# First head group's context features made among the value and receptance projections

## The chip, the cores and the metric

The kernel runs on one core of a Trainium2 chip. The metric is the device time of one execution in microseconds (us), lower is better. PE is TensorE (PEld its weight loads), DVE VectorE, ACT ScalarE, POOL GpSimd, and SP the engine that here only issues loads of weights. A queue named SP, ACT or POOL is the one on which that engine issues its DMAs.

## What is computed

The reference is a model of two blocks of two layers each, in fp32, on 256 tokens and 256 context tokens of width 1024. The change is in the second layer of the first block, whose mixer is an RWKV (a linear recurrence with a decay for each channel, in both directions, 16 heads of 64):

```python
def rwkv_features(h, ...):
    xx = centred_shift(h);  mix = lambda j: h + xx * mu[j]
    xw, xk, xv, xa = mix(1), mix(2), mix(3), mix(4)
    k = xk @ wk;  v = heads(xv @ wv)
    kk = normalized heads(k * k_k)
    for d in range(2):
        w_raw = heads(w0[d] + jnp.tanh(xw @ w1[d]) @ w2[d])
        decay = jnp.exp(-jnp.exp(-jax.nn.softplus(-w_raw) - 0.5))
        a = jax.nn.sigmoid(heads(a0[d] + (xa @ a1[d]) @ a2[d]))
        k_d = kh * (1 + (a - 1) * k_a_h)
    r = heads(mix(0) @ wr);  g = jax.nn.sigmoid(mix(5) @ g1) @ g2
# scan over the 256 context tokens from zero, then over the 256 tokens from the state left:
    S = S * w_t - (S @ kk_t) (kk_t * a_t) + v_t k_t;   y_t = S @ r_t
# both directions summed, normalized, plus a bonus, times g, then @ wo; then a residual and an MLP
```

The layer's modulation (shift, scale, gate) and that of layers behind it are products of a vector with matrices of 1024 x 6144.

## The kernel before

Products of fp32 are split into a high and a low half and made by three matmuls (lines 187 to 189); the halves of a weight tile are made by ACT (L161) and DVE (L164). Weights come as loads `wraw` on SP's queue (L151). A scheduler orders each engine's instructions beforehand; the order of the code gives it their priorities, and the pools the buffers that they wait for.

The mixer `odd1` runs in two phases. The first makes the mixes and the projections: key, value and receptance, each 1024 x 1024, with results going to memory (`kT_dram`, `kkn_dram`, `v_dram`, `rT_dram`), and three low-rank products, `lora(1)` to `twl` beside key and `lora(4)`, `lora(5)` to `tal`, `sgl` behind value. Each `lora` mixes all eight k tiles in `rw_raw` (L683) into one buffer `mixr` and then runs eight matmuls (L744).

The second phase works in four head groups: group 0 is context tokens of heads 0 to 7, group 1 the tokens of the same heads, groups 2 and 3 the same for heads 8 to 15. A group has four steps:

- **Features** (`rw_open`, then `rw_feat` for four head pairs, each with two directions; one head pair and direction is called a piece here, eight a group). A piece has two low-rank matmuls into a PSUM tile `lo` (L989) with `w2s` and `a2s`, loaded once a group on ACT's queue (L967); activations and products on ACT and DVE; four transposes of `BK` (L1046), eight products of `BK` with `ARc` (context) or `ARx` (tokens) in two tiles (L1056), and masks that write `AB` (L1069). `KB`, and `ARx` and `RB` for tokens, go to memory.
- **Inverse** (`rw_inv`): four copies of `AB` to `ND` on ACT (L1092), a transpose to `NS`, and 31 steps of two operations on DVE (L1101, L1102); then `rw_post` reassembles it on PE (L1122 and on).
- **Chain** (`rw_chain`): four steps, each with products of `UV` with `AB` (`begin`, L172), a copy `rhs` (L1214), 16 products with the inverse (L1220), the state `St`, and for tokens the outputs, which need `ard` and `rbd` reloaded.
- The next group's features are called from `ahead`, at places of a table `pos`.

Behind the chains comes the readout (L898, L938, L955), then the wo projection.

`self.side` is work of other places: twenty units of modulation products with vectors (L203). A unit is eight matmuls from four loads of 512 KB; two buffers hold them. `tick` advances it at places given by a table `tk`: at each piece of features, and after each L1220 batch. One tick is one load with its two matmuls. What is left over, `do(side)` runs behind the chains. In an execution a matmul has two records, so eight matmuls are x16 in the trace.

Of the kernel before, what the change touches and what calls it, by code (L numbers as in the profile page):

```python
# [9 lines left out]
F32 = mybir.dt.float32  # L10
# [3 lines left out]
ALU = mybir.AluOpType  # L14
# [649 lines left out]
class L1(K):  # L664
# [14 lines left out]
    def rw_raw(self, h, xx, mu, j, T):  # L679

        m = self.T(self.pp, [P, KT, T2], "mixr", bufs=1)
        for k in range(KT):
            self.nc.vector.scalar_tensor_tensor(m[:, k, :T], xx[:, k, :T], mu[:, j, k:k + 1], h[:, k, :T], ALU.mult, ALU.add)  # L683
        return m[:, :, :T]

    def odd1(self, xs, cst, Acol, Bcol):
# [27 lines left out]

        with self.phase(ns2=6) as ph:
# [17 lines left out]
            hsum = self.T(self.pp, [P, 4, 8], "hsum")  # L733
            nc.gpsimd.dma_start(hsum, A["k_hsum"])
            hexp = self.T(self.pp, [8, 4, P], "hexp")
            nc.gpsimd.dma_start(hexp, A["k_hexp"])

            def lora(j, n, T, dst):
                w = self.T(self.pp, [P, KT, P], "lw", bufs=1)
                nc.scalar.dma_start(w, A["lora1"][n])  # L740
                m = self.rw_raw(h, xx, mu, j, T)
                ps = self.psum((P, T))
                for k in range(KT):
                    nc.tensor.matmul(ps, w[:, k, :], m[:, k, :], start=k == 0, stop=k == KT - 1)  # L744
                if j == 5:
                    nc.scalar.activation(dst, ps, AF.Tanh, scale=0.5)
                    nc.vector.tensor_scalar(dst, dst, 0.5, 0.5, ALU.mult, ALU.add)
                else:
                    for d in range(2):
                        q = slice(64 * d, 64 * d + 64)  # L750
                        nc.scalar.activation(dst[q, d, :], ps[q], AF.Tanh if j == 1 else AF.Copy)

            for u in range(2):
# [3 lines left out]
                def sink(j, ps):  # L757
                    k = u * 4 + j
                    kt = self.T(self.pp, [P, T2], "kt", bufs=4)
# [10 lines left out]
                rn = self.T(self.pp, [8, T2], "rn", bufs=1)  # L770
# [3 lines left out]
                for j in range(4):  # L774
                    k = u * 4 + j
                    pb = self.T(self.pa, [P, T2], "ada")
                    nc.tensor.matmul(pb, hexp[:, j, :], rn, start=True, stop=True)
                    kn = self.S2([P, T2])
                    nc.vector.scalar_tensor_tensor(kn, kts[j], par[:, 4, k:k + 1], pb, ALU.mult, ALU.mult)
                    nc.scalar.dma_start(kknd[k], kn)  # L780
            for u in range(2):
# [10 lines left out]
            lora(4, 1, T2, tal)  # L792
            lora(5, 2, S, sgl)
            xr = self.rw_mixes(h, xx, mu, 0, S)
            for u in range(2):
                def sink(j, ps, u=u):
                    t = self.S2([P, S])
                    nc.scalar.activation(t, ps, AF.Copy)
                    nc.scalar.dma_start(rTd[u * 4 + j], t)
                self.lin_T(xr, A["wr"], u, S, sink)  # L800

# [11 lines left out]
        bon = self.T(rk, [P, 2, 16], "bon")  # L813
# [4 lines left out]
        with self.phase((3, 2, 1), 0) as ph:  # L818
# [3 lines left out]
            E3 = [self.T(gp, [P, 4, 65], f"E3{d}") for d in range(2)]  # L822
            for c in range(2):
                nc.gpsimd.memset(St[c], 0.0)
                nc.gpsimd.memset(E3[c][:, :, 64 * c:64 * c + 1], 1.0)
            E = dict(E3=E3, kT=kTd, kkn=kknd, rT=rTd, St=St, twl=twl, tal=tal, hpar=hpar, hka=hka, vd=vd,
                     ms=mstrict, mi=mincl, rmask=rmask, yd=yd, Y1=Y1, bon=bon, rkI=rkI, kbd=[self.tc.dram_tile([2, 4, P, 4, P], F32, name=f"kb_dram{g}") for g in range(4)],
                     ard=[self.tc.dram_tile([2, 4, P, 4, P], F32, name=f"ar_dram{g}") for g in range(2)],
                     rbd=[self.tc.dram_tile([2, 4, P, 8, 64], F32, name=f"rb_dram{g}") for g in range(2)])
            st = None  # L830
            self.nq = 4
            F = self.rw_open(0, False, gp)
            for hp in range(4):
                self.rw_feat(hp, gp, E, F)
            for g in range(4):
                N = {"hp": 0}

                def ahead(p):

                    while g < 3 and N["hp"] < 4 and self.pos[g][N["hp"]] <= p:  # L840
                        if N["hp"] == 0:
                            N["F"] = self.rw_open((g + 1) // 2, g % 2 == 0, gp)
# [115 lines left out]
    def rw_open(self, G, isx, gp):  # L958
# [4 lines left out]
        F["gC"] = self.T(gp, [P, 4, 2, 4], "gC", bufs=3)  # L963
# [6 lines left out]
    def rw_feat(self, hp, gp, E, F):  # L970
# [15 lines left out]
        for d in range(2):  # L986
            pwa = self.T(self.pl, [P, 2, S], "lo")
# [28 lines left out]
            ar = self.T(gp, [P, 4, P if isx else 64], "ARx" if isx else "ARc", bufs=3 if isx else 16)  # L1016
# [1069 lines left out]
```

## Time and profile before

| | us |
|---|---|
| timed runs | 2262.54, 2259.03, 2252.01 |
| their median | 2259.03 |
| the profiled execution | 2250.88 |
| its span | 2248.9 |
| PE busy in the span | 2075.3 (92%) |
| DVE, ACT, POOL busy | 1159.6, 856.6, 119.8 |

The span is what the profiler sees from the first to the last instruction. All rows below come from that one execution; their starts are us from the span's start. Stages by those starts: key about 673 to 734, value with the low-rank products to 817, receptance to 841, group 0's features to 905, the first inverse with features of groups 1 and 2 to 1014, chains to 1287, wo from 1293. Idle time of PE is what the stages are read for, since it is busy most of the span.

### The profile page before, as it was taken

To read this page: it belongs to the slowest core of one execution; us is meant where nothing else is said; L and a number is where in the kernel's file an instruction comes from. 1 tells how busy PE (TensorE), PEld (TensorE's weight loads), DVE (VectorE), ACT (ScalarE), POOL (GpSimd) and SP (SyncE) were. 2 spreads that over 40 slices of the span, in tenths; PEclk is the share of its full clock that TensorE was granted. 3 is DMA by queue.
4 is the path that set the end of the run, shared out by engine and by line. 5 is a ranking of instruction groups with operands and counts; after the bars stand their busy time and mean duration, and the time that the engine had idled before them with its cause. 6 is when DMAs were issued, how large, how long until landed. Compare 5 with 4: busy or idle time off the path is not lost. (4 is left out here: it accounts for less than half of the span.)

```text
span 2248.9 us, 32827 instructions
## 1 busy us (share of the span) xinstructions
PE 2075.3 (92%) x13114; PEld 1451.2 (65%) x13114; DVE 1159.6 (52%) x2419; ACT 856.6 (38%) x1650; POOL 119.8 (5%) x216
## 2 busy tenths in 40 slices
PE   7999899999989989899997789998998989999897
PEld 4864688888866675685652569987765439646542
DVE  2247543433465536866826265666664236475433
ACT  3334443322352446564432345544452114243211
POOL 0100000000021000001111100000000000010000
PEclk9999999999999998759897889999998999999898
DMA  7448212222332426736886555537464959452494
GB/s 285 142 186 322 76 73 94 94 94 94 113 128 89 140 100 211 228 92 200 263 280 192 177 217 183 187 118 272 171 252 163 386 202 354 156 206 96 179 383 173
DMA packets 124310, 414.53 MB, mean 184 GB/s; under 512 B 20608, under 2 KB 59152, under 8 KB 88432
## 3 DMA queue, kind: packets, MB, share of 16 engines
q1 hardware_dynamic: 59824, 340.03, 41.1%
q10 hardware_dynamic: 55552, 50.95, 7.3%
q0 software_dynamic: 8768, 21.31, 3.1%
q8 instruction: 107, 1.75, 0.3%
q14 instruction: 59, 0.48, 0.1%
HBM read 383.30 MB, written 28.93 MB: 183 GB/s over the span
## 5 line engine op out<-in xcount | busy, mean ns | idle before, releaser
L164 DVE TENSOR_TENSOR wlo<-wraw,whi 128x1024 fp32r<-128x1024 f32 x252 | 308.0, 1225 | 405.6 <-ACT whi L161 398.3
L161 ACT ACTIVATE whi<-wraw 128x1024 fp32r<-128x1024 f32 x252 | 265.4, 1058 | 490.2 <-PE mm L189 234.6
L187 PE MATMUL mm<-hT_h,whi 128*128 128x256 f32 (+1 forms) x832 | 268.2, 333 | 2.3 <-ACT whi L161 2.3
L188 PE MATMUL mm<-hT_l,whi 128*128 128x256 f32 (+1 forms) x832 | 267.3, 328 | 0.0
L189 PE MATMUL mm<-hT_h,wlo 128*128 128x256 f32 (+1 forms) x832 | 242.2, 327 | 0.5 <-DVE wlo L164 0.3
L203 PE MATMUL ada<-wraw,csil 128*32 128x512 f32 x768 | 148.1, 663 | 30.7 <-DMA wraw<-in_bda 19.7
L187 PEld LDWEIGHTS mm<-hT_h,whi 128*128 128x128 f32 x832 | 157.4, 191 | 19.8 <-ACT whi L161 4.0
L188 PEld LDWEIGHTS mm<-hT_l,whi 128*128 128x128 f32 x832 | 158.6, 191 | 14.9
L189 PEld LDWEIGHTS mm<-hT_h,wlo 128*128 128x128 f32 x832 | 149.2, 190 | 16.3 <-DVE wlo L164 1.5
L188 PE MATMUL mm<-wlo,b 128*128 128x512 f32 x384 | 151.3, 394 | 0.1
L189 PE MATMUL mm<-whi,b 128*128 128x512 f32 x384 | 150.8, 393 | 0.0
L1934 PE MATMUL ada<-wraw,mo_xd 128*64 128x512 f32 x512 | 135.5, 599 | 0.0
L187 PE MATMUL mm<-whi,b 128*128 128x512 f32 x384 | 135.1, 393 | 0.0
L310 PE MATMUL tr<-s,x 128*128 128x128 f32 x288 | 57.0, 342 | 50.4 <-DVE s L301 20.0
L188 PE MATMUL mm<-wlo,hT_h 128*128 128x512 f32 (+1 forms) x256 | 98.8, 388 | 1.4 <-DVE wlo L164 1.4
L189 PE MATMUL mm<-whi,hT_l 128*128 128x512 f32 (+1 forms) x256 | 95.9, 388 | 0.0
L187 PE MATMUL mm<-whi,hT_h 128*128 128x512 f32 (+1 forms) x256 | 95.3, 398 | 0.5 <-ACT whi L161 0.4
L310 PEld LDWEIGHTS tr<-s,x 128*128 128x128 f32 x288 | 48.9, 240 | 62.0 <-issue 33.7
L188 PEld LDWEIGHTS mm<-wlo,b 128*128 128x128 f32 x384 | 72.0, 188 | 17.9 <-DVE wlo L164 0.8
L187 PEld LDWEIGHTS mm<-whi,b 128*128 128x128 f32 x384 | 72.0, 188 | 16.6
L189 PEld LDWEIGHTS mm<-whi,b 128*128 128x128 f32 x384 | 72.0, 188 | 16.4
L1934 PEld LDWEIGHTS ada<-wraw,mo_xd 128*64 128x64 f32 x512 | 38.1, 136 | 67.9 <-issue 67.7
(520 smaller groups left out, 3714.6 us busy)
## 6 DMA issues: line engine op xcount, KB each, us to landing
wraw<-in_w SPq DMA_DIRECT2D x64, 1024.0 KB, 4.8
wraw<-in_moe_gu SPq DMA_DIRECT2D x64, 1024.0 KB, 7.8
wraw<-in_ada SPq DMA_DIRECT2D x32, 1024.0 KB, 7.2
wraw<-in_moe_d SPq DMA_DIRECT2D x32, 1024.0 KB, 7.1
wraw<-in_bda SPq DMA_DIRECT2D x48, 512.0 KB, 4.7
wraw<-in_bda SPq DMA_DIRECT2D x24, 1024.0 KB, 4.8
wraw<-in_ada SPq DMA_DIRECT2D x32, 512.0 KB, 4.8
wraw<-in_b_in SPq DMA_DIRECT2D x12, 1024.0 KB, 11.5
```

What stands on the lines that cost most here:

```text
L161: nc.scalar.activation(h, src, AF.Copy)
L164: nc.vector.tensor_tensor(l, src, h.bitcast(F32), ALU.subtract)
L187: mm(ps, ah, bh, start=first, stop=False)
L188: mm(ps, ah, bl, start=False, stop=False)
L189: mm(ps, al, bh, start=False, stop=last)
L203: i = nc.tensor.matmul(ps[q:q + 32, :], lhs[:, k, :], raw[:, j % self.wn, :], start=k < nq, stop=k >= 8 - nq, tile_position=(0, q))
L310: nc.tensor.matmul(pt[:, j, :], xs[e + j][:, k * P:(k + 1) * P], dall[:, e + j, :], start=True, stop=True)
L1934: nc.tensor.matmul(pg[64 * e:64 * e + 64, :], xd[:, k, s0:s0 + 64], gu[e](k), start=k == 0, stop=k == KT - 1, tile_position=(0, 64 * e))
```

## The change

Group 0's features (`rw_open` and four calls of `rw_feat`) are called in the first phase: two head pairs ahead of value, one behind each half of value. `lora(4)` and `lora(5)` are called ahead of value. The buffers that only key and the low-rank products use (`hsum`, `hexp`, `lw`, `mixr`, `kt`, `rn`) lie in a pool `kp`, which is released then; the features' work buffers lie in a pool `fw` that follows, released behind receptance. What outlasts the phase (`E3`, and group 0's `AB`, `gC`, `ARc`) lies in a pool `fp`, which group 3 uses again later. `rw_raw` goes; `mixr` is four buffers of one k tile. The `lo` tile of group 0's features is taken from the PSUM buffers named `ada`. The first phase has two weight buffers (`self.weights(2)`) where it had four. During the first phase `self.at` is `"end"` and `side` isn't set, so the ticks of group 0's features advance nothing; the side work begins in the second phase as `late_side`.

```diff
@@ odd1
+        fp = pool(name="fp", bufs=1)
+        E3 = [self.T(fp, [P, 4, 65], f"E3{d}") for d in range(2)]
...
+        self.weights(2)
         with self.phase(ns2=6) as ph:
...
-            hsum = self.T(self.pp, [P, 4, 8], "hsum")
+            kp = tc.alloc_tile_pool(name="kp", bufs=1, reuse_waits="tile")
+            hsum = self.T(kp, [P, 4, 8], "hsum")
...
             def lora(j, n, T, dst):
-                w = self.T(self.pp, [P, KT, P], "lw", bufs=1)
+                w = self.T(kp, [P, KT, P], "lw", bufs=1)
                 nc.scalar.dma_start(w, A["lora1"][n])
-                m = self.rw_raw(h, xx, mu, j, T)
                 ps = self.psum((P, T))
                 for k in range(KT):
-                    nc.tensor.matmul(ps, w[:, k, :], m[:, k, :], start=k == 0, stop=k == KT - 1)
+                    m = self.T(kp, [P, T2], "mixr", bufs=4)[:, :T]
+                    nc.vector.scalar_tensor_tensor(m, xx[:, k, :T], mu[:, j, k:k + 1], h[:, k, :T], ALU.mult, ALU.add)
+                    nc.tensor.matmul(ps, w[:, k, :], m, start=k == 0, stop=k == KT - 1)
...
+            lora(4, 1, T2, tal)
+            lora(5, 2, S, sgl)
+            kp.release()
+            fw = tc.alloc_tile_pool(name="fw", bufs=1, reuse_waits="tile")
+            self.pl, self.lo = self.pa, "ada"
+            F = self.rw_open(0, False, fp, fw)
+            for hp in range(2):
+                self.rw_feat(hp, fw, E, F)
             for u in range(2):
...
                 self.lin_tok(xv, A["wv"][u], range(4), sink)
-            lora(4, 1, T2, tal)
-            lora(5, 2, S, sgl)
+                self.rw_feat(2 + u, fw, E, F)
             xr = self.rw_mixes(h, xx, mu, 0, S)
...
                 self.lin_T(xr, A["wr"], u, S, sink)
+            fw.release()
...
+            self.lo = "lo"
+            self.at, self.side = "unit", self.late_side
             st = None
-            self.nq = 4
-            F = self.rw_open(0, False, gp)
-            for hp in range(4):
-                self.rw_feat(hp, gp, E, F)
...
-                            N["F"] = self.rw_open((g + 1) // 2, g % 2 == 0, gp)
+                            N["F"] = self.rw_open((g + 1) // 2, g % 2 == 0, fp if g == 2 else gp, gp)
@@ rw_open, rw_feat
-        F["AB"] = self.T(gp, [P, 64, 64], "AB", bufs=3)
+        F["AB"] = self.T(fp, [P, 64, 64], "AB", bufs=1 if fp is not gp else 2)
...
-            pwa = self.T(self.pl, [P, 2, S], "lo")
+            pwa = self.T(self.pl, [P, 2, S], self.lo)
...
-            ar = self.T(gp, [P, 4, P if isx else 64], "ARx" if isx else "ARc", bufs=3 if isx else 16)
+            ar = self.T(gp if isx else F["pool"], [P, 4, P if isx else 64], "ARx" if isx else "ARc", bufs=3 if isx else 8)
@@ layer1
-        self.at, self.side = "unit", chain(self.gates(1, 0), self.mods(1, 1), self.gates(1, 1), self.ada2(0))
+        self.at, self.late_side = "end", chain(self.gates(1, 0), self.mods(1, 1), self.gates(1, 1), self.ada2(0))
```

Lines of the features and chains stand six further down in the changed kernel (L989 is L995, L1046 L1052, L1056 L1062, L1220 L1226), L744 is L749, L798 is L810, L938 L943, L898 L903.

How the engines' rows move. PE before, behind receptance: the last receptance matmuls (L187 to L189), then the low-rank matmuls of the first pieces with side matmuls (L203) among them.

```order
L188 MATMUL mm_5665<-mixl_5527,whi_5754 128x256
L189 MATMUL mm_5665<-mixh_5526,wlo_5755 128x256
L989 MATMUL lo_5862<-twl_4498,w2s_5854 128x256
L989 MATMUL lo_5862<-tal_4499,a2s_5856 128x256
L203 MATMUL ada_5869<-wraw_5870,csil_6_86 32x512 x2
L989 MATMUL lo_5919<-twl_4498,w2s_5854 128x256
L989 MATMUL lo_5919<-tal_4499,a2s_5856 128x256
L989 MATMUL lo_5975<-twl_4498,w2s_5854 128x256
L989 MATMUL lo_5975<-tal_4499,a2s_5856 128x256
L1046 MATMUL tr_5895<-ident_67,BK_5890 128x128 x4
L1056 MATMUL tr_5903<-ARc_5891,BK_5890 128x64 x4
```

These L989, L1046 and L1056 are group 0's; in the changed kernel none of them is left here.

PE after, in the second half of the value projection (`mm` and `mixh` are value's product and mix): a piece's low-rank matmuls, transposes and products now lie between its rows.

```order
L995 MATMUL ada_5372<-twl_4498,w2s_5228 128x256
L995 MATMUL ada_5372<-tal_4499,a2s_5230 128x256
L189 MATMUL mm_5417<-whi_5508,mixl_5102 128x512
L187 MATMUL mm_5418<-whi_5508,mixh_5101 128x512
L188 MATMUL mm_5418<-wlo_5509,mixh_5101 128x512
L1052 MATMUL tr_5260<-ident_67,BK_5255 128x128 x4
L1062 MATMUL tr_5268<-ARc_5256,BK_5255 128x64 x4
L189 MATMUL mm_5418<-whi_5508,mixl_5102 128x512
L187 MATMUL mm_5419<-whi_5508,mixh_5101 128x512
L188 MATMUL mm_5419<-wlo_5509,mixh_5101 128x512
L189 MATMUL mm_5419<-whi_5508,mixl_5102 128x512
```

Eight pieces stand so among value and receptance, and no L203 stands among them. The first row behind receptance is an L172 on `UV`, sixteen in all, and then L995 of group 1.

ACT before, behind receptance (L798 are its last copies): the loads of `w2s` and `a2s`, then those of the first features.

```order
L798 ACTIVATE s_1145_5788<-mm_5664 128x256
L798 ACTIVATE s_1146_5791<-mm_5665 128x256
L967 DMA w2s_5854<-in_w2s 128x512
L799 DMA rT_dram<-s_1145_5788 128x256
L799 DMA rT_dram<-s_1146_5791 128x256
L967 DMA a2s_5856<-in_a2s 128x512
L980 DMA kTl_5858<-kT_dram 128x256
L982 DMA kknl_5860<-kkn_dram 128x256
L980 DMA kTl_5971<-kT_dram 128x256
L982 DMA kknl_5973<-kkn_dram 128x256
```

The first UV load (L1178) follows these, and the `ND` copies stood some 60 us further on.

ACT after, at the same place (L810 are the same copies, `ND` the copies for the first inverse, `UV` the first chain's start):

```order
L810 ACTIVATE s_1278_6210<-mm_6086 128x256
L810 ACTIVATE s_1279_6213<-mm_6087 128x256
L1098 ACTIVATE ND_6262<-AB_5226 32x1024 x4
L1184 DMA UV_6514<-v_dram_4505 64x512
L811 DMA rT_dram<-s_1278_6210 128x256
L811 DMA rT_dram<-s_1279_6213 128x256
L1184 DMA UV_6516<-v_dram_4506 64x512
L1184 DMA UV_6600<-v_dram_4505 64x512
L1184 DMA UV_6602<-v_dram_4506 64x512
L973 DMA w2s_6631<-in_w2s 128x512
L973 DMA a2s_6633<-in_a2s 128x512
```

The `ND` copies and the `UV` loads have moved ahead of `w2s` and `a2s`, which are now group 1's.

SP before, at the end of the chains (`in_bda0` are side loads of 512 KB, `in_wo` and `in_w1_1` weights of 1 MB):

```order
L151 DMA wraw_1831_8777<-in_bda0 128x1024
L151 DMA wraw_1832_8781<-in_bda0 128x1024
L151 DMA wraw_2172_10632<-in_wo 128x2048
L151 DMA wraw_2177_10666<-in_wo 128x2048
L151 DMA wraw_2182_10700<-in_wo 128x2048
L151 DMA wraw_2187_10734<-in_wo 128x2048
L151 DMA wraw_2240_10910<-in_w1_1 128x2048
L151 DMA wraw_2245_10968<-in_w1_1 128x2048
```

Here the whole side work has been loaded before wo.

SP after, at the same place:

```order
L151 DMA wraw_1963_9475<-in_bda0 128x1024
L151 DMA wraw_1975_9518<-in_bda0 128x1024
L151 DMA wraw_2194_10668<-in_wo 128x2048
L151 DMA wraw_2199_10702<-in_wo 128x2048
L151 DMA wraw_2204_10736<-in_wo 128x2048
L151 DMA wraw_2209_10770<-in_wo 128x2048
L151 DMA wraw_2262_10947<-in_w1_1 128x2048
L151 DMA wraw_2267_11005<-in_w1_1 128x2048
L151 DMA wraw_1991_9578<-in_bda0 128x1024
L151 DMA wraw_1992_9582<-in_bda0 128x1024
L151 DMA wraw_2280_11087<-in_w1_1 128x2048
```

Two side loads, `wraw_1991` and `wraw_1992`, now stand behind four loads of wo and two of the MLP.

PE before, behind the last L1220 batch (the L172 end its outputs):

```order
L172 MATMUL mm_10426<-UV_10341,rbd_10347 64x64
L172 MATMUL mm_10426<-UV_10343,rbd_10351 64x64
L938 MATMUL tr_10574<-y_1_1152_5818,rwc_4484 128x512
L955 MATMUL tr_10589<-g_1154_5820,sgl_4504 128x512
L187 MATMUL mm_10628<-whi_10634,moh_2148_10555 128x512
L187 MATMUL mm_10629<-whi_10634,moh_2148_10555 128x512
L938 MATMUL tr_10593<-y_1_1152_5818,rwc_4484 128x512
L188 MATMUL mm_10628<-wlo_10635,moh_2148_10555 128x512
L189 MATMUL mm_10628<-whi_10634,mol_2150_10557 128x512
```

The wo projection follows the outputs with only the readout's L938 and L955 between.

PE after, at the same place; the last two L203 use those two side loads (here without the first of their numbers):

```order
L217 MATMUL ada_9468<-adp_9466,sel_4_76 2x512
L203 MATMUL ada_9474<-wraw_9475,csil_16_107 32x512 x2
L203 MATMUL ada_9474<-wraw_9518,csil_16_107 32x512 x2
L203 MATMUL ada_9474<-wraw_9578,csil_16_107 32x512 x2
L203 MATMUL ada_9474<-wraw_9582,csil_16_107 32x512 x2
L217 MATMUL ada_9604<-adp_9602,sel_4_76 2x512
L903 MATMUL tr_10595<-ident_67,z_1281_6237 128x128 x4
L903 MATMUL tr_10602<-ident_67,z_1281_6237 128x128 x4
L187 MATMUL mm_10664<-whi_10670,moh_2170_10591 128x512
L188 MATMUL mm_10664<-wlo_10671,moh_2170_10591 128x512
L187 MATMUL mm_10665<-whi_10670,moh_2170_10591 128x512
```

Side matmuls, their selections (L217) and eight transposes of `z` (L903) now stand ahead of the wo projection, where it came after readout rows. In all, of the 160 side matmuls in PE's row, 32 stood ahead of the first L1220 batch and none behind the sixteenth; now none stands ahead of the first, and twelve behind the sixteenth. L1122, the first inverse's reassembly, stood behind some 14 pieces of groups 1 and 2, and now behind nine. At the first L1220 batch all 16 context pieces and half a token piece of group 3 had been passed, now 12.

## Rows read from the trace of the kernel before

**Rows 1.** The windows view by stage: busy us (instructions) per engine, TensorE's granted clock, DMA share, GB/s.

```profile
734.00:817.00 83.00, 79.43 (x275) 50.55 (x275) 36.45 (x50) 32.97 (x49) 0.00 (x0) 0.98 0.38 135
...
841.00:905.00 64.00, 56.16 (x304) 35.04 (x304) 37.03 (x89) 37.70 (x101) 3.90 (x8) 0.84 0.72 226
...
1014.00:1287.00 273.00, 233.72 (x3331) 139.09 (x3331) 148.30 (x351) 100.10 (x178) 36.77 (x69) 0.89 0.72 226
1287.00:1314.00 27.00, 19.55 (x114) 14.23 (x114) 21.26 (x31) 14.93 (x21) 0.00 (x0) 0.95 0.87 359
```

**Rows 2.** The timeline of PE behind receptance: start us, duration us, instruction, [idle before <-releaser].

```profile
840.30 0.28 PE L189 MATMUL mm<-mixh,wlo 128*128 128x256 f32 x1
844.23 1.19 PE L989 MATMUL lo<-twl,w2s 128*128 128x256 f32 x2 [3.65 <-DMA w2s<-in_w2s]
847.18 1.19 PE L989 MATMUL lo<-tal,a2s 128*128 128x256 f32 x2 [1.77 <-DMA a2s<-in_a2s]
```

**Rows 3.** The timeline of PE in the first group's features, one piece.

```profile
873.68 0.70 PE L989 MATMUL lo<-twl,w2s 128*128 128x256 f32 x2
...
874.75 1.10 PE L1056 MATMUL tr<-ARc,BK 64*128 64x64 f32 x8
875.78 0.66 PE L1046 MATMUL tr<-ident,BK 128*128 128x128 f32 x4
```

**Rows 4.** The timeline of PE in the second context group's features, one piece.

```profile
966.61 1.22 PE L989 MATMUL lo<-twl,w2s 128*128 128x256 f32 x2
...
968.61 1.97 PE L1056 MATMUL tr<-ARc,BK 64*128 64x64 f32 x8
970.51 1.11 PE L1046 MATMUL tr<-ident,BK 128*128 128x128 f32 x4
```

**Rows 5.** The windows view of three other stretches.

```profile
867.00:918.00 51.00, 48.92 (x328) 32.22 (x329) 38.61 (x101) 34.85 (x87) 4.68 (x9) 1.00 0.83 252
...
967.00:1017.00 50.00, 49.50 (x435) 40.59 (x438) 32.48 (x83) 32.09 (x66) 1.11 (x2) 0.50 0.27 76
...
1293.00:1314.00 21.00, 16.21 (x65) 11.66 (x64) 19.97 (x29) 10.20 (x14) 0.00 (x0) 0.93 1.01 424
```

**Rows 6.** The timeline of DVE in the value projection: six of a low-rank mix's operations.

```profile
744.36 4.05 DVE L683 SCALAR_TENSOR_TENSOR mixr<-xx,mu,h 128x512 f32<-128x512 f32 x6
```

**Rows 7.** The timeline of ACT: the four copies ahead of the first inverse.

```profile
903.38 3.18 ACT L1092 ACTIVATE ND<-AB 32x1024 f32<-32x1024 f32 x3
...
906.57 1.05 ACT L1092 ACTIVATE ND<-AB 32x1024 f32<-32x1024 f32 x1
```

**Rows 8.** Groups of PE by line, 905 to 986: busy us, mean ns | idle before.

```profile
L1056 PE MATMUL tr<-ARx,BK 64*128 64x128 f32 x121 | 21.7, 355 | 1.0 <-ACT KB L1049 0.5 <-DVE bon L1041 0.4
L1056 PE MATMUL tr<-ARc,BK 64*128 64x64 f32 x88 | 15.6, 358 | 0.1
```

**Rows 9.** The timeline of PE: the inverse's reassembly, and the first chain step.

```profile
985.85 1.92 PE L1122 MATMUL post<-NS,AB 32*32 32x32 f32 x64
...
1014.65 1.97 PE L1220 MATMUL mm<-rhs,AB 64*64 64x64 f32 x30
```

**Rows 10.** Line L203 in 1000 to 1290: durations, and what PE and PEld waited for.

```profile
L203 PE MATMUL ada<-wraw,csil x256: 589/617/1062, 1016.5 to 1255.1; 128*32 128x512 f32 x128
...
  DMA wraw<-in_bda: 43.8, 26
  DMA wraw<-in_ada: 9.6, 13
```

**Rows 11.** The timeline of PE from the last chain step to the wo projection.

```profile
1285.79 1.15 PE L1220 MATMUL mm<-rhs,AB 64*64 64x64 f32 x32 [0.75 <-ACT rhs L1214]
...
1288.24 1.15 PE L172 MATMUL mm<-UV,rbd 128*64 128x64 f32 x30 [0.17 <-ACT UV L1224]
...
1293.30 1.02 PE L187 MATMUL mm<-whi,moh 128*128 128x512 f32 x2
```

**Rows 12.** The timeline of SP's queue: the loads of wo.

```profile
1267.97 22.73 SPq L151 DMA_DIRECT2D wraw<-in_wo  x4
```

More of the change, by code (lines that the diff above doesn't have):

```diff
@@ L677, in rw_mixes @@
         return [self.rw_mix1(*a, k) for k in range(KT)].__getitem__
[L679 to L684, printed above, removed]
     def odd1(self, xs, cst, Acol, Bcol):
@@ L713, in odd1 @@
         vd = [self.tc.dram_tile([T2, D], F32, name=f"v_dram{d}") for d in range(2)]
+        fp = pool(name="fp", bufs=1)
+        E3 = [self.T(fp, [P, 4, 65], f"E3{d}") for d in range(2)]
+        for d in range(2):
+            nc.gpsimd.memset(E3[d][:, :, 64 * d:64 * d + 1], 1.0)
+        bon = self.T(rk, [P, 2, 16], "bon")
+        E = dict(E3=E3, kT=kTd, kkn=kknd, rT=rTd, twl=twl, tal=tal, hpar=hpar, hka=hka, vd=vd, ms=mstrict, mi=mincl, rmask=rmask, bon=bon, rkI=rkI,
+                 kbd=[self.tc.dram_tile([2, 4, P, 4, P], F32, name=f"kb_dram{g}") for g in range(4)],
+                 ard=[self.tc.dram_tile([2, 4, P, 4, P], F32, name=f"ar_dram{g}") for g in range(2)],
+                 rbd=[self.tc.dram_tile([2, 4, P, 8, 64], F32, name=f"rb_dram{g}") for g in range(2)])
+        self.weights(2)
         with self.phase(ns2=6) as ph:
@@ L732, in odd1 @@
             xk = xk.__getitem__
-            hsum = self.T(self.pp, [P, 4, 8], "hsum")
+            kp = tc.alloc_tile_pool(name="kp", bufs=1, reuse_waits="tile")
+            hsum = self.T(kp, [P, 4, 8], "hsum")
             nc.gpsimd.dma_start(hsum, A["k_hsum"])
-            hexp = self.T(self.pp, [8, 4, P], "hexp")
+            hexp = self.T(kp, [8, 4, P], "hexp")
             nc.gpsimd.dma_start(hexp, A["k_hexp"])
             def lora(j, n, T, dst):
-                w = self.T(self.pp, [P, KT, P], "lw", bufs=1)
+                w = self.T(kp, [P, KT, P], "lw", bufs=1)
                 nc.scalar.dma_start(w, A["lora1"][n])
-                m = self.rw_raw(h, xx, mu, j, T)
                 ps = self.psum((P, T))
                 for k in range(KT):
-                    nc.tensor.matmul(ps, w[:, k, :], m[:, k, :], start=k == 0, stop=k == KT - 1)
+                    m = self.T(kp, [P, T2], "mixr", bufs=4)[:, :T]
+                    nc.vector.scalar_tensor_tensor(m, xx[:, k, :T], mu[:, j, k:k + 1], h[:, k, :T], ALU.mult, ALU.add)
+                    nc.tensor.matmul(ps, w[:, k, :], m, start=k == 0, stop=k == KT - 1)
                 if j == 5:
@@ L758, in sink @@
                     k = u * 4 + j
-                    kt = self.T(self.pp, [P, T2], "kt", bufs=4)
+                    kt = self.T(kp, [P, T2], "kt", bufs=4)
                     nc.scalar.activation(kt, ps, AF.Copy)
@@ L769, in odd1 @@
                     lora(1, 0, T2, twl)
-                rn = self.T(self.pp, [8, T2], "rn", bufs=1)
+                rn = self.T(kp, [8, T2], "rn", bufs=1)
                 nc.vector.tensor_scalar(rn, pn, 1e-24, None, ALU.max)
@@ L812, in odd1 @@
         yd = [self.tc.dram_tile([S, 512], F32, name=f"y_dram{d}") for d in range(2)]
-        bon = self.T(rk, [P, 2, 16], "bon")
         rk2 = pool(name="rk2", bufs=1)
@@ L821, in odd1 @@
             St = [self.T(gp, [P, 2, 4, P], f"St{c}") for c in range(2)]
-            E3 = [self.T(gp, [P, 4, 65], f"E3{d}") for d in range(2)]
             for c in range(2):
                 nc.gpsimd.memset(St[c], 0.0)
[L825 to L829, printed above, removed]
+            E.update(St=St, yd=yd, Y1=Y1)
+            self.lo = "lo"
+            self.at, self.side = "unit", self.late_side
             st = None
-            self.nq = 4
-            F = self.rw_open(0, False, gp)
-            for hp in range(4):
-                self.rw_feat(hp, gp, E, F)
             for g in range(4):
@@ L956, in rw_readout, with rw_open @@
         tt(z, ps, z, ALU.mult)
-    def rw_open(self, G, isx, gp):
+    def rw_open(self, G, isx, fp, gp):
         nc = self.nc
         F = {"G": G, "x": isx}
-        F["AB"] = self.T(gp, [P, 64, 64], "AB", bufs=3)
+        F["AB"] = self.T(fp, [P, 64, 64], "AB", bufs=1 if fp is not gp else 2)
+        F["pool"] = fp
         F["g"] = G * 2 + isx
-        F["gC"] = self.T(gp, [P, 4, 2, 4], "gC", bufs=3)
+        F["gC"] = self.T(fp, [P, 4, 2, 4], "gC", bufs=1 if fp is not gp else 2)
         F["AR"] = {}
```

## The prediction

> **What bounds the kernel now.** I read the stages first, then TensorE's timeline at their borders, then the waits of the side work and the load queue. From the value projection to the end of the head groups TensorE is the engine that works on: it is busy 79 of 83 us in the projections, 56 of 64 while the first group's context features are made, 234 of 273 in the chains, and 20 of 27 behind them [rows 1]. So the kernel gets shorter only where TensorE idles less, where its instructions run at the higher clock, or where work finds idle time. The 64 us from 841 to 905 are what the change takes apart: eight pieces (four head pairs, two directions) of features, and 16 side ticks, which are the modulation products of later layers (L203), each fed by a load of 512 KB.
>
> At the border TensorE ends receptance at 840.58, starts the first feature at 844.23 after 3.65 us for w2s, and waits 1.77 us more for a2s [rows 2]: some 7.7 us from the last projection matmul to 848.4, where it runs on without a wait. A context piece costs about 3.8 us at the higher clock: 1.07 us for its four low-rank matmuls (873.68 to 874.75), 1.03 us for half of its L1056 products, twice, and 0.66 for its transposes [rows 3]. At the lower clock it is 2.00 + 2 x 1.90 + 1.11 = 6.9 us [rows 4]. Both clocks occur: the granted clock is 1.00 in 867 to 918 and 0.50 in 967 to 1017, that is 2.4 and 1.2 GHz [rows 5].
>
> **Step 1, the pieces move into the projections.** Eight pieces at 3.8 us are 30 us that now lie among value and receptance, where TensorE is kept busy; the order shows them spread between L187 to L189. Their ACT and DVE work has room: DVE is busy 36 of 83 us and ACT 33 there [rows 1]. Little of their TensorE time hides, since only 3.6 us of those 83 are idle. Two low-rank products are pulled ahead of value, and 16 mixes for them, at 0.68 us each on DVE (4.05 us for six, [rows 6]), about 11 us, now stand ahead of some value mixes. TensorE can meanwhile work on what is already mixed; I take 4 us of stall, with 0 and 11 as the ends. So receptance ends near 840.6 + 30.4 + 4 = 875 instead of 840.6.
>
> **Step 2, the border.** ACT's row changes: ahead of w2s and a2s now stand four ND copies of the first inverse and the four UV loads. The copies took 3.18 and 1.05 us [rows 7]. TensorE waits for all of this, since its next work is 16 products on UV and then group 1's low-rank matmuls; behind the copies ACT's queue also holds back the loads of kT, kkn and rT that group 1 needs. I add the 4.2 us of copies to the 7.7 us of before: 12 us from receptance to free running, 887. The ends are 8 (the copies start before the last rT stores are issued) and 16 (the copies wait for the last piece's AB on DVE as well).
>
> **Step 3, group 1 and the first inverse.** From 887 the inverse's 31 steps on DVE run beside group 1's eight query pieces; the reassembly L1122 stands in TensorE's row behind 8.75 pieces. In the row of before, the stretch from 905 to 986 made 121 products on ARx and 88 on ARc, sixteen records a piece, so 7.6 + 5.5 = 13.1 pieces in 81 us, 6.2 us each [rows 8]. That stretch has both clocks. After a border of 12 idle us I expect the lower one first, as before, where the first L989 pair behind receptance took 1.19 us [rows 2] and a later one 0.70 [rows 3]; I take 6.6 us, nearer to the 6.9 of [rows 4] than to the 3.8 of [rows 3]. 8.75 x 6.6 = 58 us gives 945 for the reassembly, where it was 985.85. From there to the first chain step it was 28.8 us [rows 9]; three pieces of group 2 stand between them now and about two before, so 35 us. The first chain step comes at 980 instead of 1014.65: **-35 us**. With the ends of the steps (0 and 11, 8 and 16, 3.8 and 6.9 us a piece) it is -70 to -20, but 3.8 for all pieces is a case of its own below; without it, -42 to -20.
>
> **Step 4, what is owed in the chains.** At the first chain step 12 of the 16 context pieces stand in TensorE's row, where it was all 16 and half a query piece more. These 4.5 pieces now lie in the chains, at 3.8 us since the clock is back there: **+17 us**. The side work is owed too: at the first chain step it has done 0 of its 160 matmuls, where it had 32, and by the last step 148 instead of 160. So 20 matmuls more lie between the first step and the last, 10 loads. Two ended waits show what a load costs there: 43.8 + 9.6 us over 64 loads in weight loads and matmuls together, 0.83 us a load, and 256 records at 0.617 us median that run four abreast, 0.6 us a load [rows 10]. 10 x 1.4 = **+14 us**. Against both stand the 39.3 us in which TensorE is idle in the chains [rows 1]; most of it is these very load waits, so I let only 11 us be filled: **-11 us**, with 0 and 25 as ends. The last chain step then comes some 15 us earlier than 1285.79 [rows 11].
>
> **Step 5, the end.** Twelve side matmuls stand behind the last chain step, and the last two of their loads stand on SP's queue behind four loads of wo and two of w1. Before, no side load stood behind wo. SP issued the four wo loads over 22.73 us from 1267.97, so that all but the first waited until about 1289 to 1290.7 for room that the head groups' buffers give back [rows 12]. In 1293 to 1314 the engines moved 424 GB/s [rows 5], 2.5 us for one load of 1 MB. Three of wo and two of w1 go first, then the two halves: six times 2.5 is 15 us from the release, 1305 on the clock of before. Then come four matmuls, a copy, a selection, and eight transposes that only now prepare the wo projection, for some 6 us, where from L172 to the projection it was 1288.24 to 1293.30 with the readout in between [rows 11]. Projection starts at 1311 to 1314 instead of 1293.30, **+20 us**. The ends: +5 if the first loads already left by the time of the release, +27 if the clock falls in the wait.
>
> **Two smaller parts.** K now runs with two weight buffers of 1 MB instead of four, and the context buffers are split into two pools. In 734 to 817 the DMA share is 0.38 [rows 1], so two buffers should feed it: 0, from -2 to +3.
>
> The sum is -35 + 17 + 14 - 11 + 20 = **+5 us**. It is made on the profiled execution, 2250.88 us, span 2248.9, which lies under the lowest of the three timed runs; the step is an addition, so I set it on their median: 2259 + 5 = **2264 us**.
>
> **Rivals.** (A) Group 1 runs at the higher clock: 8.75 pieces at 4.4 instead of 6.6 us, 20 us less, 2244 us. Deciding is whether the clock comes back behind the 12 idle us. For it: 867 to 918 held 1.00 at 49 of 51 us busy. Against it: 967 to 1017 held 0.50 although TensorE was busy 49.5 of 50 us [rows 5]. The Trainium skill, page "TensorE: Matmul & The Clock Gate", section "What's actually happening", gives the lower clock to an idle TensorE and the higher to a busy one. By that rule the step would be case A; the trace disagrees in 967 to 1017, and agrees in 867 to 918.
> (B) Slower: the owed side work finds no idle time. Two 512 KB buffers feed it, each refilled only after its matmuls; with a tick for more of the chain the load wait follows every one. Then the 11 us are not filled and each of the 10 loads costs some 0.8 us more: +19, 2283 us. It decides where the loads' landing, and not TensorE, sets the distance of two ticks. For it: most of the idle time of the chains before already ended on a load [rows 10].
> (C) The pieces in value wait for DVE, whose mixes, scans and products now come together: 12 us more, 2276 us. Against it, DVE's 36 of 83 us [rows 1].
> (D) The end costs half, since the two late loads leave with the first of wo: -10, 2254 us.
>
> **How the numbers follow.** The forecast has 0.42, A 0.20, B 0.20, C 0.10, D 0.08. About half a per cent, 11 us, is what a measurement of this kernel can tell from no change. Faster than 2248 are two thirds of A and a little of the forecast's spread of some 14 us: 0.18. Slower than 2270 are B, most of C and a quarter of the forecast: 0.38. The rest, 0.44, is within. The range takes A's and B's centres with a little room: 2242 to 2286.
>
> **What would show it.** Receptance ending near 875 with the pieces among its rows at 3.8 us; first L995 of group 1 some 10 us behind it; the reassembly near 945 and the first L1226 batch near 980; L203 absent before that batch; last batch near 1271; then a wait of TensorE on a bda load of 10 us or more, and wo starting at about 1298. The forecast is wrong if the last batch comes before 1255 (A), after 1285 (B), or if no wait on a load stands between it and wo (D).

## The result

The change makes the kernel about one per cent slower: 2281.35 us in the median (2278.87 to 2291.61) against 2260.78, ratio 1.0107 with an interval of 1.0064 to 1.0149. Timed again beside later runs it gave 1.0134 (1.0076 to 1.0191). The profiled execution took 2283.19 us, span 2281.4; it stands 32.5 us of span behind that of before. The medians differ by 20.6, since the profiled execution of before lies under the four timed ones that stand beside it, and that of the changed kernel above its median.

The stages in the changed kernel's windows (busy us of PE, PEld, DVE, ACT, POOL, then clock, DMA share, GB/s): value with its pieces, the first group of token features, the chains, and the stretch from the last chain step to the wo projection; they answer to [rows 1].

```profile
734.00:775.00 41.00, 35.57 (x93) 18.30 (x92) 27.64 (x41) 12.71 (x18) 0.00 (x0) 0.88 0.29 100
775.00:875.00 100.00, 97.65 (x560) 79.92 (x559) 48.52 (x94) 53.57 (x116) 5.00 (x9) 0.97 0.40 133
980.00:1283.00 303.00, 258.72 (x3458) 156.87 (x3460) 165.19 (x399) 116.03 (x218) 36.26 (x68) 0.88 0.72 224
1283.00:1317.00 34.00, 14.77 (x86) 5.14 (x87) 4.36 (x5) 6.58 (x10) 2.63 (x5) 0.70 0.97 379
876.00:951.00 75.00, 58.90 (x291) 46.36 (x292) 61.16 (x173) 37.58 (x99) 0.00 (x0) 0.62 0.59 175
```

TensorE is idle for 5.4 us at the border of key and value and then works on, at a clock near full, for 100 us with the eight pieces in it. From 876 to 951 the clock is 0.62. The chains are 303 us long, and behind them TensorE works 15 of 34 us while the DMA engines are busy 97% of the time. Now the same places in TensorE's timeline, which answer to [rows 2, 9, 11]: receptance's end and the first token piece, the reassembly, the first and the last chain step, and the way to wo.

```profile
881.74 0.44 PE L172 MATMUL mm<-UV,AB 64*64 64x64 f32 x2 [6.42 <-DMA UV<-v_dram]
884.75 1.22 PE L995 MATMUL lo<-twl,w2s 128*128 128x256 f32 x2
...
949.97 1.27 PE L1128 MATMUL post<-NS,AB 32*32 32x32 f32 x39
...
978.83 1.14 PE L1226 MATMUL mm<-rhs,AB 64*64 64x64 f32 x30 [0.45 <-ACT AB L1137]
...
1281.83 1.15 PE L1226 MATMUL mm<-rhs,AB 64*64 64x64 f32 x32 [0.75 <-ACT rhs L1220]
...
1308.83 3.19 PE L203 MATMUL ada<-wraw,csil 128*32 128x512 f32 x8 [16.18 <-DMA wraw<-in_bda]
1312.78 1.86 PE L217 MATMUL ada<-adp,sel 128*2 128x512 f32 x2 [0.76 <-ACT adp L209]
1314.57 1.97 PE L903 MATMUL tr<-ident,z 128*128 128x128 f32 x8
1316.38 0.63 PE L187 MATMUL mm<-whi,moh 128*128 128x512 f32 x1
```

The first chain step comes 35.8 us earlier than before, the last only 4.0 us earlier, and wo starts 23.1 us later. So 31.9 us go back in the chains and 27 behind them. From wo to the norm behind it another 3 us are lost, and some 6 us in the layers behind it, which were not there when the changed kernel was profiled a second time (917.7 us from that norm to the end, 917.1 in the kernel before): I take that for the difference of two executions, and no part of the change. That second profile has the first chain step at 979.25, the last at 1286.96 and wo at 1322.21, so its chains are 307.7 us long. A difference of some 5 us between two single profiles explains nothing by itself.

### The profile page after: what moved, and what is told of

Same layout as the page of the kernel before. It is cut to its first block, busy times and chain, and to the rows that moved or that the text cites. A ratio compares the mean times of both kernels' runs of the same rounds, so it can differ in the third digit from the quotient of the medians.

```text
span 2281.4 us, 32827 instructions
## 1 busy us (share of the span) xinstructions
PE 2072.4 (91%) x13114; PEld 1450.4 (64%) x13114; DVE 1159.6 (51%) x2419; ACT 855.8 (38%) x1650; POOL 113.4 (5%) x216
## 5 line engine op out<-in xcount | busy, mean ns | idle before, releaser
L187 PE MATMUL mm<-hT_h,whi 128*128 128x256 f32 (+1 forms) x832 | 268.1, 334 | 2.3 <-ACT whi L161 2.3
L189 PE MATMUL mm<-hT_h,wlo 128*128 128x256 f32 (+1 forms) x832 | 243.0, 328 | 0.8 <-DVE wlo L164 0.6
L203 PE MATMUL ada<-wraw,csil 128*32 128x512 f32 x768 | 149.8, 671 | 38.2 <-DMA wraw<-in_bda 30.2
L187 PEld LDWEIGHTS mm<-hT_h,whi 128*128 128x128 f32 x832 | 157.6, 192 | 19.8 <-ACT whi L161 3.7
L189 PEld LDWEIGHTS mm<-hT_h,wlo 128*128 128x128 f32 x832 | 149.8, 191 | 16.8 <-DVE wlo L164 2.4
L189 PE MATMUL mm<-whi,b 128*128 128x512 f32 x384 | 150.8, 393 | 0.0
L187 PE MATMUL mm<-whi,b 128*128 128x512 f32 x384 | 135.1, 393 | 0.0
L187 PE MATMUL mm<-whi,hT_h 128*128 128x512 f32 (+1 forms) x256 | 95.3, 398 | 0.5 <-ACT whi L161 0.4
L189 PE MATMUL mm<-whi,hT_l 128*128 128x512 f32 (+1 forms) x256 | 95.3, 385 | 0.0
L187 PEld LDWEIGHTS mm<-whi,b 128*128 128x128 f32 x384 | 72.0, 188 | 16.7
L189 PEld LDWEIGHTS mm<-whi,b 128*128 128x128 f32 x384 | 72.0, 188 | 16.4
```

The lines of the kernel that those rows point to most:

```text
L187: mm(ps, ah, bh, start=first, stop=False)
L189: mm(ps, al, bh, start=False, stop=last)
L203: i = nc.tensor.matmul(ps[q:q + 32, :], lhs[:, k, :], raw[:, j % self.wn, :], start=k < nq, stop=k >= 8 - nq, tile_position=(0, q))
```

## Experiments

Each run was timed on the same chip as the kernel before; ratios are to that kernel.

**The two late loads.** On SP's queue, all loads of wo but the first, and those behind them, are made to follow the last side load.

```diff
     def wload(self, ap):
         t = self.T(self.wr, [P, self.wn, 512], "wraw")
-        (self.wq or self.nc.sync).dma_start(t, ap)
+        self.lastload = (self.wq or self.nc.sync).dma_start(t, ap)
+        if self.tail is not None:
+            self.nwo += 1
+            if self.nwo > 1:
+                self.after(self.lastload, self.tail)
...
             self.do(self.side)
+            self.tail = self.lastload
```

> The changed kernel with one edit of order: on SP's queue all loads of wo but the first, and the first of the MLP, follow the last side load. Theory (the two late loads wait for 5 MB queued ahead of them): the wait of 16.2 us on a bda load falls under 4 us, wo starts at about 1302 instead of 1316.4, and the whole is 13 to 15 us less, about 2267 us, 1.003 of before. Rival (the wait only moves to wo's own loads, which now start later): TensorE waits 10 us or more on whi or wlo of wo, and the whole is 0 to 4 us less, about 2279 us, 1.008.

Measured: 1.0077 (1.0042 to 1.0111), some 7 to 13 us under the changed kernel's 1.0107 and 1.0134. The intervals overlap, and the total is the rival's 1.008 rather than the theory's 1.003; it is the trace that decides between them. In the timeline behind its last chain step (1282.50) the wait of 16.18 us has become two of less than 3:

```profile
1294.25 1.05 PE L211 MATMUL ada<-wraw,csil 128*32 128x512 f32 x4 [2.81 <-DMA wraw<-in_bda]
1298.04 3.26 PE L211 MATMUL ada<-wraw,csil 128*32 128x512 f32 x8 [2.74 <-DMA wraw<-in_bda]
1303.85 1.88 PE L912 MATMUL tr<-ident,z 128*128 128x128 f32 x8
1305.65 0.50 PE L195 MATMUL mm<-whi,moh 128*128 128x512 f32 x1
```

The rival that the wait only moves to wo falls: wo starts 10.7 us earlier, and TensorE has no long wait on its weights. But from the last step it is still 23 us to wo, against 7.5 before and 34.6 in the changed kernel. So the queue's order is 11 of the 27 us lost at the end. The other 16 go with the six loads of side work that stand there at all, with their matmuls, copies and selections one after the other.

**Putting the side work off, alone.** The kernel before, with the ticks of group 0's features advancing nothing.

```diff
-        self.at, self.side = "unit", chain(self.gates(1, 0), ...)
+        self.at, self.late_side = "end", chain(self.gates(1, 0), ...)
...
             for hp in range(4):
                 self.rw_feat(hp, gp, E, F)
+            self.at, self.side = "unit", self.late_side
```

> The kernel before with one part of the change: the ticks of group 0's features advance nothing, the side work begins behind them. Features stay where they were. Two side loads stand behind wo and two of the MLP's loads, as in the changed kernel. Theory (putting the side work off costs most of what the change lost): the first chain step comes 4 to 9 us earlier than 1014.65, the sixteen steps take 285 to 295 us instead of 270, a wait of 13 to 17 us on a bda load stands ahead of wo; 2282 us, 1.010 of before (1.006 to 1.013). Rival (side work fills idle time wherever it stands, the loss is in the moved features): within 5 us of before, 1.000.

Measured: 1.0299 (1.0245 to 1.0353), 66 us, far more than either theory said. First chain step 1021.02, last 1313.55, wo 1365.96. The chains took 292.5 us, as expected, and the end 52 instead of 7.5: nine loads, not six, are left behind the last step.

```profile
1339.96 3.18 PE L203 MATMUL ada<-wraw,csil 128*32 128x512 f32 x8 [14.49 <-DMA wraw<-in_bda]
1352.57 3.13 PE L203 MATMUL ada<-wraw,csil 128*32 128x512 f32 x8 [7.64 <-DMA wraw<-in_bda]
...
1365.96 0.80 PE L187 MATMUL mm<-whi,moh 128*128 128x512 f32 x1
```

The nine loads make the total depend on this run's order too. The first chain step came 6 us later, though 32 side matmuls and one and a half pieces less stood ahead of it. The window shows a likely reason, which the next run looks at: at 841 to 905 the granted clock was 0.53, where with side matmuls it is 0.84 [rows 1].

```profile
841.00:905.00 64.00, 56.74 (x208) 43.55 (x208) 33.29 (x79) 34.05 (x96) 0.43 (x1) 0.53 0.40 119
```

**Matmuls without loads in their place.** The same kernel, with 32 matmuls of the side work's shape on a tile that is at hand instead of the dead ticks; they compute nothing that is used.

```diff
+        for _ in range(n if self.fillr is not None else 0):
...
+                i = self.nc.tensor.matmul(self.fps[q:q + 32, :], self.cs[:, k, :], self.fillr, start=k < 4, stop=k >= 4, tile_position=(0, q))
+                self.after(i, after)
```

> The kernel of e3_before_late (the kernel before, side work begun behind group 0's features) with 32 matmuls in the place of the ticks that do nothing: the same shape as side matmuls, from a tile that is at hand, without a load, their result unused. Side work stays as late as in e3_before_late, two side loads stand behind wo. Theory (without side matmuls the features alone do not hold the higher clock): the granted clock from 841 to 905 rises from 0.53 to 0.75 or more, group 0's features end earlier although there is more to do, the first chain step comes at 1010 or earlier instead of 1022; 10 to 15 us less than e3_before_late, about 1.024 of before. Rival (the clock there does not depend on them, e3_before_late lost its time to late loads alone): clock 0.53 to 0.60, first chain step at 1022 to 1030, 1.030 or more.

Measured: 1.0195 (1.0119 to 1.0271); the first chain step at 1022.62.

```profile
841.00:905.00 64.00, 56.25 (x270) 34.05 (x270) 30.68 (x76) 31.67 (x90) 0.54 (x1) 0.76 0.39 116
```

Half of it held. The clock did rise, from 0.53 to 0.76, and TensorE did 270 instead of 208 records in the same busy time; 56 of the 62 more are the fill itself. But the first step didn't come earlier. Its own row had changed as well: with the fill, 16 context and 9 token pieces stand ahead of that step, instead of 15 and 8. So 32 matmuls, whose rows cover 16.2 us, and two pieces more cost 1.6 us; what the clock alone is worth in this kernel was not separated from that. The order behind the first step changed too: the chains take 259.6 us instead of 292.5, and the end 64.6 instead of 52.4, with 13 loads behind the last step (1282.18, wo 1346.83). So its ratio says little on the clock.

**Side work put back.** The changed kernel with ticks at the start of the second phase: 8, 16 or 32.

```diff
             self.at, self.side = "unit", self.late_side
+            self.tick(16)
             st = None
```

> The changed kernel with 16 ticks of side work (32 matmuls, four units) issued at the start of the second phase, as many as the kernel before has done by its first chain step. In SP's row no side load stands behind wo any more. Theory (the loss is the side work that was put off): first chain step 5 to 9 us later than the changed kernel's 978.8 (four units at 2.1 us, part of it in the border's idle time), the sixteen steps take 275 to 285 us instead of 303, no wait of 16 us at the end, wo starts near 1293 to 1297; about 2257 us, 0.998 of before. Rival (the chains got longer because of the deferred context pieces and DVE, not of the side work): the sixteen steps still take about 300 us, only the wait at the end goes, about 2268 us, 1.003.

> The changed kernel with 8 ticks of side work (two units) at the start of the second phase; in SP's row no side load stands behind wo. Theory (the gain of 16 ticks has two parts, the late loads at the end, and the higher clock that side matmuls bring to the first features): the wait at the end goes, the granted clock from 876 to 951 lies between the 0.62 of the changed kernel and the 0.75 of 16 ticks, 2250 to 2262 us, 0.998 to 1.003 of before. Rival (all of it is the late loads): as fast as with 16 ticks, 0.990 to 0.993.

> The changed kernel with 32 ticks (eight units) at the start of the second phase. In the order 44 side matmuls stand ahead of the first chain step, where 16 ticks put 32. Theory (side work ahead of the first step is paid back in the chains, and keeps the clock): clock from 876 to 951 at 0.75 or more, first chain step within 5 us of the 973 of 16 ticks, 0.986 to 0.992 of before. Rival (two buffers of 512 KB feed it, so the features wait on loads): first chain step at 980 or later, 0.993 to 1.000.

> The changed kernel again, beside the runs below on the same chip. Every theory: 1.008 to 1.015 of before.

| ticks put back | ratio (interval) | first step | last step | wo | clock 876 to 951 |
|---|---|---|---|---|---|
| 0 (the changed kernel, again) | 1.0134 (1.0076 to 1.0191) | 978.8 | 1281.8 | 1316.4 | 0.62 |
| 8 | 0.9939 (0.9913 to 0.9964) | 977.5 | 1265.3 | 1275.3 | 0.66 |
| 16 | 0.9906 (0.9877 to 0.9934) | 971.7 | 1273.2 | 1282.1 | 0.75 |
| 32 | 0.9911 (0.9871 to 0.9951) | 971.0 | 1269.3 | 1276.8 | 0.76 |

Times and clock in the first row are those of the trace above. One line of code turns a loss of 1.2 per cent into a gain of 0.9. From the last step to wo it is 9.9, 8.9 and 7.5 us, where it was 7.5 before and 34.6 in the changed kernel, so the first 8 ticks do that already; for that part the rival of the run with 8 ticks is right, and its theory's 0.998 too high. Its 0.9939 lies between the two forecasts. The expectation for 16 ticks had the total too high (2257 expected, 2234 measured), and was wrong on the way: the first chain step came earlier, not later, and the chains did not get shorter. They take 301.5 us.

```profile
971.65 1.60 PE L1227 MATMUL mm<-rhs,AB 64*64 64x64 f32 x30
...
1273.20 1.15 PE L1227 MATMUL mm<-rhs,AB 64*64 64x64 f32 x32 [0.75 <-ACT rhs L1221]
...
1282.09 1.33 PE L187 MATMUL mm<-whi,moh 128*128 128x512 f32 x2
```

The order tells it: with 16 ticks 8 of the 16 context pieces stand ahead of the first step, where it was 12 in the changed kernel and 16 before. With as much side work ahead of the chains as the kernel before has, the chains are 30.4 us longer and hold eight context pieces and one token piece more, 3.4 us each if all of it is theirs. That agrees with the run's rival, but it is a price fitted to one run and not shown. The run with 8 ticks does not fit it: its chains hold six and a half pieces and eight loads more than those of the kernel before, and are only 16.7 us longer (287.9). The run with 32 ticks came as its theory had it. In the clock column the granted clock rises with the side matmuls put back. With 16 ticks it does so although TensorE is busy for less of the stretch than the 58.90 us of the changed kernel:

```profile
876.00:951.00 75.00, 57.20 (x268) 32.04 (x268) 57.58 (x160) 36.22 (x88) 3.04 (x6) 0.75 0.83 252
```

**UV on another queue.** The changed kernel, and the one with 16 ticks, with the UV loads on POOL's queue.

```diff
-    qs = dict(..., uv="scalar", ...)
+    qs = dict(..., uv="gpsimd", ...)
```

> The changed kernel with the UV loads on POOL's queue instead of ACT's, where they stood behind the four ND copies. The scheduler's other choices follow: in SP's row no side load stands behind wo now. Theory (the border's 6.4 us wait for UV comes from ACT's row, and the tail from the late loads): the wait behind receptance falls to 2 us or less, the first L995 starts at 880 to 881 instead of 884.8, first chain step 973 to 976, no wait above 5 us ahead of wo; about 2263 us, 1.001 of before. Rival (UV's own landing sets the wait, and the tail is paid by longer chains): the wait stays at 5 us or more, the sixteen steps take 310 us or more; about 2277 us, 1.007.

> The kernel of e1_side16 (the changed kernel with 16 ticks at the start of the second phase) with the UV loads on POOL's queue. In the order 14 of 16 context pieces now stand ahead of the first chain step instead of 8. Theory (pieces ahead of the first step and pieces in the chains cost about the same): first chain step 990 to 1000 instead of 973, the sixteen steps 280 to 285 us instead of 301, 0.988 to 0.994 of before. Rival (pieces ahead of the first step cost more there, at the lower clock): 0.995 to 1.002.

On the changed kernel: 1.0129 (1.0078 to 1.0181), nothing gained. The 6.42 us wait for UV gave way to waits on w2s and a2s; the first L995 started 8.8 us earlier (4.1 of it because receptance ended earlier), and yet the first chain step came 7.6 us later (986.47), with 14 context pieces ahead of it instead of 12. No late load stood behind wo.

```profile
875.99 1.22 PE L995 MATMUL lo<-twl,w2s 128*128 128x256 f32 x2 [4.80 <-DMA w2s<-in_w2s]
880.71 1.22 PE L995 MATMUL lo<-tal,a2s 128*128 128x256 f32 x2 [3.50 <-DMA a2s<-in_a2s]
```

So the border's wait, which I had given 12 us in the sum, does not set the first chain step by itself. The run changes the order in many places, and its chains took 323 us, so it isn't clean; I don't draw more from it. On the kernel with 16 ticks: 0.9956 (0.9925 to 0.9987), first step 1001.12, last 1277.68. Six context pieces and half a token piece more ahead of the first step cost 29.5 us there and saved 25.0 in the chains: 4.5 us a piece ahead, 3.8 in the chains. The rival's interval fits better than the theory's, by a small margin.

**More side work without the move.** The kernel before, with 16 ticks ahead of group 0's features on top of those within them.

```diff
+            self.tick(16)
             F = self.rw_open(0, False, gp)
```

> The kernel before with 16 ticks of side work ahead of group 0's features, on top of those within them: 64 side matmuls stand ahead of the first chain step instead of 32. Features stay where they were. Theory (moving the features is what gains once the side work is not put off): the first chain step 5 to 12 us later than 1014.65, the chains as much shorter, 0.996 to 1.003 of before. Rival (more side work ahead of the chains is what gained 0.9 per cent, with or without the move): 0.988 to 0.994.

Measured: 0.9922 (0.9894 to 0.9949), as much as the best with the move; the rival is right. First step 9.3 us later (1023.94), and the sixteen steps 248.6 us instead of 271.1.

```profile
1023.94 1.97 PE L1221 MATMUL mm<-rhs,AB 64*64 64x64 f32 x30
...
1272.55 1.15 PE L1221 MATMUL mm<-rhs,AB 64*64 64x64 f32 x32 [0.75 <-ACT rhs L1215]
...
1280.06 1.03 PE L187 MATMUL mm<-whi,moh 128*128 128x512 f32 x2
```

By count of side matmuls ahead of the first step, features in their old place: none 1.0299, 32 1.000, 64 0.9922. Features moved: none 1.011 to 1.013, 16 0.9939, 32 0.9906, 44 0.9911. So at equal side work the move gains: 0.9 per cent at 32, and 1.7 to 1.9 at none, where the old place also left nine loads behind the last step and the new one six. What the change lost, it lost through the side work that it put off with the move. With enough side work ahead of the chains, either place of the features ends at about 0.99.

## Why the prediction was right, and where not

It put 2264, 2242 to 2286; measured were 2281.35, inside, on the slower side of it. I held no measurable change for a little likelier than slower, and it is slower. The sum had +5 us, the medians moved by 20.6: that the range holds them it owes to rival B's 2283, near which I had set its end, and not to the sum.

- *Step 1.* Receptance was to end at 875; its last matmul starts at 875.04. The eight pieces cost what [rows 3] say: TensorE's busy time from 734 to receptance's end grew by 30.7 us for 30.4. Its idle time in 734 to 875 is 7.8 us by the two windows, where [rows 1] leave 3.6 until 817. So the 4 us of stall held in size, but by luck: I had charged them to the mixes on DVE, and 4.9 us of TensorE's idle time there ended on the loads of the low-rank weights (`lw`).
- *Step 2.* TensorE was to run on freely from 887; the first L995 came at 884.75 and the next piece's, behind one more wait of 1.28 us, at 888.06. The wait is for UV, behind the copies on ACT's queue, as the order had it.
- *Step 3.* The reassembly at 945 came at 949.97, the first chain step at 980 at 978.83. The lower clock that I chose was granted for the most part (0.62, and 0.55 on a second profile): case A, with the features at the higher clock, did not come. My reason, the idle border, does not carry it: with 16 ticks put back TensorE was idle for longer in this stretch, and the clock was 0.75. And I had the pieces without a wait, where 9.5 of the 63 us from 887 to the reassembly are idle, most of them waits for ACT's and DVE's results. By the Trainium skill's page "TensorE: Matmul & The Clock Gate", section "What's actually happening", a busy engine has the higher clock; the trace disagrees most plainly in the run that puts the side work off alone, 0.53 at 56.7 us busy of 64.
- *Step 4, the step that failed.* The two debts came to the right size, 17 + 14 = 31 us where 31.9 came back. The 11 us that I let idle time fill are the error. The chains' rows show most of both debts as busy time:

```profile
L203 PE MATMUL ada<-wraw,csil 128*32 128x512 f32 x296 | 77.0, 699 | 19.4 <-DMA wraw<-in_bda 11.8 <-DMA wraw<-in_ada 7.4 <-DVE adb L271 0.2
L172 PE MATMUL mm<-UV,KBl 128*64 128x64 f32 x448 | 23.5, 253 | 9.3 <-ACT UV L1230 9.3
L1062 PE MATMUL tr<-ARc,BK 64*128 64x64 f32 x64 | 6.9, 278 | 0.0
```

  In the kernel before it is these rows, and no row of ARc at all:

```profile
L203 PE MATMUL ada<-wraw,csil 128*32 128x512 f32 x256 | 68.3, 694 | 28.7 <-DMA wraw<-in_bda 19.7 <-DMA wraw<-in_ada 3.6 <-DVE bB L255 2.4
L172 PE MATMUL mm<-UV,KBl 128*64 128x64 f32 x448 | 20.5, 236 | 0.5 <-ACT UV L1224 0.5
```

  Forty records more are the 10 loads, and the 64 of ARc four pieces. TensorE's busy time in the chains went from 233.7 [rows 1] to 258.7 us, its idle time from 39.3 to 44.3: in sum none of it was filled. Of the 39.3 us, 23.3 ended on the very loads that were to fill it, and I counted them as room all the same. With ten loads more the idle time at the side matmuls even fell, from 28.7 to 19.4 us; but the rest rose from 10.6 to 24.9, and most of that is two waits of 2.55 and 6.70 us for ACT's copy of `UV`. Why these came is open.

  The price of 1.4 us a load is borne out by the last experiment, where 16 loads less in the chains made them 22.5 us shorter, 1.4 each. But its two terms were wrong, and their errors cancelled. [rows 10] adds up the waits of PE and of PEld, which wait for the same loads: TensorE itself was idle for 23.3 us before 64 loads, 0.36 each and not 0.83. And the 256 records cover 68.3 us, 1.07 a load and not 0.6. So three quarters of the price is work, and one quarter waiting.
- *Step 5.* The mechanism was right and the size small: 27 us for 20, its upper end, which I had tied to the clock falling in the wait. It fell to 0.70 in the stretch, but that is the smaller part: from the landing to wo it is 7.6 us where I had some 6. The rest is the landing itself. SP's queue shows the loads leave:

```profile
1286.70 2.74 SPq L151 DMA_DIRECT2D wraw<-in_wo  x4
1289.48 1.79 SPq L151 DMA_DIRECT2D wraw<-in_w  x2
1291.38 1.64 SPq L151 DMA_DIRECT2D wraw<-in_bda  x2
```

  All four loads of wo, and not three, left when the room came, and from there to the landing at 1308.8 it is 22 us where I had 15. The engines moved 379 GB/s in 1283 to 1317, not the 424 of [rows 5]. And the last chain step was not 15 but 4 us earlier, so wo came 23.1 us later and not 5.
- *Rival B* gave nearly the measured time, 2283, for half its reason. In sum no idle time was filled, but a load in the chains did not get dearer: the side matmuls' waits on loads came to 0.36 us a load before and 0.26 after. *C* falls with step 1. *D* falls with the 16.18 us wait.
- What I missed altogether is that the granted clock of the stretch that the side matmuls leave depends on them, as the last section shows. Read from the rows of before alone, their absence looked like less work for TensorE.

## What to carry to other kernels

When work moves ahead, ask what was woven into the place that it leaves: here a stream of small loads with matmuls, whose amount ahead of the next bound stage was worth more than the move. The idle time of a stage is no room by its sum: here the waits on the loads shrank when ten loads more came, and others grew by more. And a wait that stands in two engines' rows is to be counted once. A late small load behind large ones on one queue waited here for their whole transfer; look in the order for such a load before the engines' times.

## What the runs showed of the hardware

The granted clock of a stretch of small matmuls depended on what stood among them, at like busy time. At 841 to 905, behind receptance, TensorE was busy 56 to 57 of 64 us in three kernels: with no side matmuls the clock was 0.53, with 28 that need no load 0.76, and with those of the kernel before 0.84. In the kernel before with 16 more ticks receptance ends 10 us later, and the same stretch, 851 to 915, has 0.87 at 55.6 us busy, so the extra ticks add little:

```profile
851.00:915.00 64.00, 55.64 (x320) 36.08 (x321) 35.80 (x90) 41.84 (x109) 1.60 (x3) 0.87 0.77 238
```

A shorter window shows the two levels, 1.2 and 2.4 GHz, by themselves. These are 889 to 905 in the run that puts the side work off alone, and in the run with matmuls in its place:

```profile
889.00:905.00 16.00, 16.00 (x64) 13.22 (x63) 9.22 (x24) 8.02 (x23) 0.43 (x1) 0.50 0.30 90
889.00:905.00 16.00, 16.00 (x102) 9.54 (x100) 11.83 (x30) 10.11 (x31) 0.54 (x1) 1.00 0.46 136
```

TensorE is busy in all of both, by the profile, at the lower level in the first and at the higher in the second. A value between is a mean over a stretch that has both. So a busy share does not tell the clock; the profile's clock column does. What such a rise is worth in time stays open: more work ran in the same time, but no run moved the clock without moving the order.
